# A unit's value products in one row behind all of its transposes, last block of keys first

## The chip, the cores and the metric

The kernel runs on one core of a Trainium2 chip. The metric is the device time of one launch in microseconds; the time before is the median of three runs. Inside a core, TensorE (PE in the profile; PEld is its weight load) multiplies, VectorE (DVE), ScalarE (ACT) and GpSimd (POOL) do the rest, and SyncE (SP) issues the transfers.

## The reference

Two decoder layers over 512 tokens of width 1024. A layer projects the residual stream, runs two kinds of attention side by side, projects their outputs back, normalises, and runs a gated feed-forward part. What matters here are the two kinds of attention:

```python
# kind "a": sliding window of 128 with sinks, 8 query heads, 2 key/value heads
pr = jnp.exp(s - m)
denom = pr.sum(-1, keepdims=True) + jnp.exp(sink - m)
o = jnp.einsum('bnhgqk,bnkhd->bnqhgd', (pr / denom).astype(v.dtype), vv)
# kind "b": the 128 best keys of each query by an indexer's score, 8 query heads, 1 key/value head
_, sel = lax.top_k(idx_score, k_top)
ks, vs = gather(k, sel), gather(v, sel)
pr = jax.nn.softmax(s, axis=-1)
o = jnp.einsum('bqhgj,bqjhd->bqhgd', pr.astype(v.dtype), vs)
```

The kernel doesn't gather: it masks the scores of kind "b" outside the 128 best keys, so both kinds are a masked softmax followed by probabilities times values.

## The kernel before

Tokens are worked on in four tiles of 128. In a layer, `start()` projects the indexer's columns, keys and values and the first queries; `index()` makes the indexer's scores; then three streams are woven into one program order by `Order.run`: `rest()` (the other queries, then the output projection of kind "a" through `from_ma`), `attention()` and `topk()`. Each stream yields the estimated cost of what it has just issued, and the stream with the least accumulated cost goes next. That order is a priority: when the program is built, the framework replays it on a model of the engines, and where an instruction isn't ready on its engine there, a later one that is ready goes ahead. On the chip each engine then runs its own list strictly in order.

Attention is cut into 16 units a layer: kind "a" or "b", a tile t of queries, a group g of four heads. Kind "a" looks at one block of 128 keys (t = 0) or two, kind "b" at t + 1 blocks. `scores` of a unit makes the masked scores (L684, PE), their row minimum (L688, DVE) and the exponentials (L692, ACT); two units later `values` follows, woven step by step with the scores of a later unit. For each block of keys, `values` transposes the four heads' probabilities on PE into a PSUM bank (L721, four 128x128 transposes), copies them to a tile of SBUF (L723, ACT), and multiplies them with the values: `pv(b)` (L715), two matmuls with 64 columns of values as the stationary operand, one for each half of the output's 128 partitions, so each uses half of the array's columns. In float32 a matmul of L715 stands in the trace as two records, so one `pv(b)` is four records. All blocks add into one PSUM accumulator `o`. Then the reciprocals of the sums are transposed (L732) and copied (L735), and DVE scales `o` by them (L740); L747 and L748 split the result in two parts.

Before the change, `pv(b)` is issued `LAG` blocks behind the transposes: one for kind "a", two for kind "b", and the last ones behind L732; after each there is a yield, at which other streams and the scores come in. The copied probabilities lie in `t2k()`, a pool of 12 tiles that also holds the exponentials. `slot()` is another pool, of 28 tiles: keys, queries, values, the outputs of kind "a", and the tiles into which SP loads quarters of `w_down` ahead (L232).

Products of the projections go through `mm3` (L325 to L327), three matmuls over 128 rows and 128 columns of the array.

Of the kernel before, what the change touches and what calls it, by code (L numbers as in the profile page):

```python
# [10 lines left out]
F32 = mybir.dt.float32  # L11
# [24 lines left out]
NSLOT, NTMP = 28, 12  # L36
D_GI, D_KI, D_K, D_Q, AHEAD = 9.0, 13.0, 8.0, 10.0, 2
IDX_PACE, NSTART, R_MAIN, R_TOP = 1.5, 2, 0.75, 0.001
LAG, FILL = dict(a=1, b=2), {2: 6, 5: -2}
QS = [("a", 0), ("a", 1), ("b", 0), ("b", 1)]  # L40


# [54 lines left out]
def hybrid_kernel(ctx: ExitStack, tc: tile.TileContext, x, p, positions, ln_in_g, ln_in_b, w_in,  # L97
# [15 lines left out]
    def bank(tag, bufs, dt=F32):  # L113
        return psum.tile([128, 512], dt, name="bank", tag="bank", bufs=8)

    def acc():
        return bank("acc", 4)

    def slot(dt=F32R):
        return slots.tile([128, 512], dt, name="slot", tag="slot")  # L120

    def t2k(dt=F32):
        return tmp.tile([128, 512], dt, name="t2k", tag="t2k")
# [224 lines left out]
    def tok(t):  # L348
        return slice(t * 128, (t + 1) * 128)
# [198 lines left out]
    for l in range(L):  # L548
# [84 lines left out]
        def wait(*keys):  # L633
            while not all(k in ready for k in keys):
                yield None
# [67 lines left out]
        def values(kind, t, g, st):  # L703

            es, rb, b0, nb = st
            c = g if kind == "a" else 2
            o = acc()[:, :256].rearrange("p (a n) -> p a n", a=2)
            pts = {}
            lag, cost = LAG[kind], 0.45
            if kind == "b":  # L710
                yield from wait("x read")

            def pv(b):
                for u in range(2):
                    PE.matmul(o[u * 64:(u + 1) * 64], vt[b0 + b][:, c * 64:(c + 1) * 64], pts[b][:, u],  # L715
                              start=b == 0, stop=b == nb - 1)

            for b in range(nb):
                ps = bank("tp", 2)
                for j in range(4):  # L720
                    PE.transpose(ps[:, j * 128:(j + 1) * 128], es[j][:, b * 128:(b + 1) * 128], idf)  # L721
                pt = t2k()
                A.copy(pt, ps)  # L723
                pts[b] = pt.rearrange("p (a u n) -> p u a n", a=2, u=2)
                yield 0.44
                if b >= lag:
                    pv(b - lag)
                    yield cost

            pr = bank("tp", 2)  # L730
            for a in range(2):
                PE.transpose(pr[:, a * 128:(a + 1) * 128], rb[:, a * 128:(a + 1) * 128], idf)  # L732
            tt = t2k()
            rr, of = (tt[:, i * 256:(i + 1) * 256].rearrange("p (a n) -> p a n", a=2) for i in range(2))
            A.copy(rr, pr[:, :256].rearrange("p (a n) -> p a n", a=2))  # L735
            yield 0.44
            for b in range(max(0, nb - lag), nb):
                pv(b)
                yield cost
            V.tensor_tensor(of, o, rr, OP.mult)  # L740
            if kind == "a":
                m = ma[t, g] = slot().rearrange("p (s a n) -> p s a n", s=2, a=2)
                hi, lo = m[:, 0], m[:, 1]
            else:
                k = 4 + 2 * g
                hi, lo = fh[:, k:k + 2, tok(t)], fl[:, k:k + 2, tok(t)]
            A.copy(hi, of)  # L747
            G.tensor_tensor(lo, of, hi, OP.subtract)  # L748
            ready.add(("m" + kind, t, g))
# [3 lines left out]
        def attention():  # L753

            st = {}
            for i in range(len(units) + AHEAD):
                gs = []
                if i in FILL:
                    yield 0.0, FILL[i]
                if i < len(units):  # L760
                    st[i] = []
                    gs.append(scores(*units[i], st[i]))
                if i >= AHEAD:
                    gs.append(values(*units[i - AHEAD], st.pop(i - AHEAD)))
                while gs:
                    none = True
                    for g in list(gs):
                        try:
                            c = next(g)
                        except StopIteration:  # L770
                            gs.remove(g)
                            none = False
                            continue
                        if c is not None:
                            none = False
                            yield c
                    if none:
                        yield None
# [230 lines left out]
        for b in TAIL:  # L1009
            for h in range(2):  # L1010
# [18 lines left out]
                for i, t in enumerate(b):  # L1029
                    a = t2k()  # L1030
# [37 lines left out]
```

## Time and profile before

| | us |
|---|---|
| median of 3 runs | 1252.13 (1251.35 to 1252.41) |
| profiled execution | 1251.81, its span 1249.7 |
| PE busy | 1225.9 (98%) |
| DVE, POOL, ACT busy | 765.2, 682.9, 576.4 |
| attention and what is woven with it, layer 1 | about 95 to 218 us of the span |
| the same, layer 2 | about 705 to 830 us of the span |

An engine's busy time is the union of its instructions. A matmul's row spans its way through the array, and successive matmuls overlap, so what a matmul costs is the step from its start to the start of the next one and not the length of its row.

### The profile page before, as it was taken

To read this page: it belongs to the slowest core of one execution; us is meant where nothing else is said; L and a number is where in the kernel's file an instruction comes from. 1 tells how busy PE (TensorE), PEld (TensorE's weight loads), DVE (VectorE), ACT (ScalarE), POOL (GpSimd) and SP (SyncE) were. 2 spreads that over 40 slices of the span, in tenths; PEclk is the share of its full clock that TensorE was granted. 3 is DMA by queue.
4 is the path that set the end of the run, shared out by engine and by line. 5 is a ranking of instruction groups with operands and counts; after the bars stand their busy time and mean duration, and the time that the engine had idled before them with its cause. 6 is when DMAs were issued, how large, how long until landed. Compare 5 with 4: busy or idle time off the path is not lost.

```text
span 1249.7 us, 18006 instructions
## 1 busy us (share of the span) xinstructions
PE 1225.9 (98%) x6552; PEld 1029.9 (82%) x6552; DVE 765.2 (61%) x1678; ACT 576.4 (46%) x1193; POOL 682.9 (55%) x555
## 2 busy tenths in 40 slices
PE   7999999999999999999999999999999999999996
PEld 5998777988888888888899987689888888888885
DVE  7699954682727272726677998286555555555365
ACT  6577763442434343433337787534343333333331
POOL 6885532566566666663169754234757575757400
PEclk9999999999999999999999999999999999999999
DMA  5232311333232323034033203114323333321321
GB/s 177 78 92 85 95 42 35 119 118 118 85 118 84 118 85 118 18 118 140 2 89 114 101 21 117 52 54 149 99 87 105 97 105 99 103 83 52 101 84 50
DMA packets 89264, 112.74 MB, mean 90 GB/s; under 512 B 5460, under 2 KB 66132, under 8 KB 89176
## 3 DMA queue, kind: packets, MB, share of 16 engines
q1 hardware_dynamic: 88504, 111.58, 28.5%
q8 instruction: 51, 0.84, 0.3%
q14 instruction: 37, 0.30, 0.1%
q10 hardware_dynamic: 672, 0.03, 0.0%
HBM read 109.49 MB, written 2.10 MB: 89 GB/s over the span
## 4 chain that ended last, share of the span: by engine, by line
PE 82%; POOL 5%; DVE 3%; issue 3%; ACT 3%; DMA 3%; SPq 0%; DVEq 0%; ACTq 0%; POOLq 0%
PE bank L325 24%; PE bank L326 24%; PE bank L327 24%; PE bank L715 3%; PE bank L684 3%; PE bank L721 2%; POOL wsp L279 2%; DMA wst<-in_w_pg_dram 2%; POOL wsp L257 1%; PE bank L523 1%; PE bank L438 1%; PE bank L732 1%; ACT wsp L278 1%; DVE slot L273 1%; POOL slot L517 1%
## 5 line engine op out<-in xcount | busy, mean ns | idle before, releaser
L279 POOL TENSOR_TENSOR wsp<-wst,wsp 128x1024 fp32r<-128x1024 f32 (+2 forms) x148 | 351.3, 2389 | 244.4 <-ACT wsp L278 240.8
L326 PE MATMUL bank<-fl,wsp 128*128 128x512 f32 (+1 forms) x768 | 284.8, 372 | 0.4 <-DVE fl L441 0.4
L325 PE MATMUL bank<-fh,wsp 128*128 128x512 f32 (+1 forms) x768 | 283.6, 372 | 1.0 <-ACT fh L440 1.0
L327 PE MATMUL bank<-fh,wsp 128*128 128x512 f32 (+1 forms) x768 | 283.1, 371 | 0.0
L278 ACT CAST wsp<-wst 128x1024 fp32r<-128x1024 f32 (+2 forms) x148 | 151.6, 1033 | 166.4 <-PE bank L327 126.2
L325 PE MATMUL bank<-wsp,fh 128*128 128x256 f32 (+3 forms) x512 | 165.2, 326 | 3.6 <-DVE work L648 2.0
L874 DVE TENSOR_TENSOR t2k<-bank,t2k 128x512 f32<-128x512 f32 x44 | 30.4, 692 | 222.0 <-PE bank L327 222.0
L326 PEld LDWEIGHTS bank<-fl,wsp 128*128 128x128 f32 x768 | 144.6, 188 | 25.7 <-DVE fl L441 0.9
L325 PEld LDWEIGHTS bank<-fh,wsp 128*128 128x128 f32 x768 | 143.6, 188 | 26.8 <-ACT fh L440 1.9
L327 PEld LDWEIGHTS bank<-fh,wsp 128*128 128x128 f32 x768 | 144.6, 188 | 24.9
L327 PE MATMUL bank<-wsp,fl 128*128 128x256 f32 (+3 forms) x512 | 163.7, 322 | 1.4 <-DVE fl L441 0.8
L326 PE MATMUL bank<-wsp,fh 128*128 128x256 f32 (+3 forms) x512 | 164.7, 322 | 0.0
L257 POOL TENSOR_TENSOR wsp<-slot,wsp 128x512 fp32r<-128x512 f32 x100 | 141.6, 1442 | 29.0 <-ACT wsp L256 29.0
L325 PE MATMUL bank<-wsp,slot 128*128 128x512 f32 x392 | 153.8, 392 | 0.0
L326 PE MATMUL bank<-wsp,slot 128*128 128x512 f32 x392 | 152.7, 390 | 0.0
L327 PE MATMUL bank<-wsp,slot 128*128 128x512 f32 x392 | 148.4, 390 | 0.0
L790 DVE TENSOR_TENSOR x<-bank,x 128x512 f32<-128x512 f32 x140 | 91.5, 684 | 88.5 <-PE bank L327 88.5
L904 ACT CAST slot<-t2k 128x256 fp32r<-128x256 f32 (+1 forms) x104 | 49.8, 497 | 144.1 <-DVE t2k L874 102.5
L257 POOL TENSOR_TENSOR wsp<-t2k,wsp 128x512 fp32r<-128x512 f32 x40 | 57.5, 1448 | 92.4 <-ACT wsp L256 92.4
L325 PEld LDWEIGHTS bank<-wsp,fh 128*128 128x128 f32 x512 | 97.6, 191 | 11.9 <-ACT fh L440 2.4
L327 PEld LDWEIGHTS bank<-wsp,fl 128*128 128x128 f32 x512 | 97.5, 191 | 7.9 <-DVE fl L441 1.1
L326 PEld LDWEIGHTS bank<-wsp,fh 128*128 128x128 f32 x512 | 98.0, 191 | 6.5 <-issue 1.2
(152 smaller groups left out, 2004.6 us busy)
## 6 DMA issues: line engine op xcount, KB each, us to landing
wst<-in_w_gu_dram SPq DMA_DIRECT2D x88, 512.0 KB, 3.5
slot<-in_w_down_dram SPq DMA_DIRECT2D x80, 256.0 KB, 2.8
wst<-in_w_in_dram SPq DMA_DIRECT2D x16, 512.0 KB, 3.6
wst<-in_w_o_dram SPq DMA_DIRECT2D x16, 512.0 KB, 3.8
wst<-in_w_pg_dram SPq DMA_DIRECT2D x16, 512.0 KB, 4.2
wst<-in_w_in_dram SPq DMA_DIRECT2D x8, 256.0 KB, 2.7
lng<-in_ln_g_dram SPq DMA_DIRECT2D x4, 512.0 KB, 4.8
lnb<-in_ln_b_dram SPq DMA_DIRECT2D x4, 512.0 KB, 5.5
```

The source lines that it names most:

```text
L257: G.tensor_tensor(w[:, 1, j], src[j], w[:, 0, j], OP.subtract)
L278: A.copy(w[:, 0, :a * n], st[:, :a * n])
L279: G.tensor_tensor(w[:, 1, :a * n], st[:, :a * n], w[:, 0, :a * n], OP.subtract)
L325: PE.matmul(o, sh, mh, start=start, stop=False, skip_group_check=again)
L326: PE.matmul(o, sh, ml, start=False, stop=False, skip_group_check=again)
L327: PE.matmul(o, sl, mh, start=False, stop=stop, skip_group_check=again)
L684: PE.matmul(ps[:, o:o + nn], qT[kind, t, g][:, j * 128:(j + 1) * 128], kT[c, s][:, k0:k0 + nn], start=(s == 0), stop=(s == 1))
L715: PE.matmul(o[u * 64:(u + 1) * 64], vt[b0 + b][:, c * 64:(c + 1) * 64], pts[b][:, u], start=b == 0, stop=b == nb - 1)
L721: PE.transpose(ps[:, j * 128:(j + 1) * 128], es[j][:, b * 128:(b + 1) * 128], idf)
L790: V.tensor_tensor(xt[t][:, c], ps, xt[t][:, c], OP.add)
L874: V.tensor_tensor(a, ps[1, f], a, OP.mult)
L904: A.copy(h[0], src)
```

## The change

`LAG` goes. In `values` all blocks are transposed and copied first, then come the reciprocals' transposes (L732) and their copy, and behind them all `pv(b)` of the unit without a yield between, from the last block to the first; the accumulation starts with the last block and stops with the first. For kind "b" the copied probabilities move from `t2k()` to `slot()`, since up to four of them live at once. The yields are 0.44 for each block, 0.22 behind L732 and 0.2 + 0.45 per block behind the products; before they were 0.44 for each block, 0.44 behind L732 and 0.45 behind each product.

```diff
-LAG, FILL = dict(a=1, b=2), {2: 6, 5: -2}
+FILL = {2: 6, 5: -2}
...
-            lag, cost = LAG[kind], 0.45
...
             def pv(b):
                 for u in range(2):
                     PE.matmul(o[u * 64:(u + 1) * 64], vt[b0 + b][:, c * 64:(c + 1) * 64], pts[b][:, u],
-                              start=b == 0, stop=b == nb - 1)
+                              start=b == nb - 1, stop=b == 0)
 
             for b in range(nb):
                 ps = bank("tp", 2)
                 for j in range(4):
                     PE.transpose(ps[:, j * 128:(j + 1) * 128], es[j][:, b * 128:(b + 1) * 128], idf)
-                pt = t2k()
+                pt = slot(F32) if kind == "b" else t2k()
                 A.copy(pt, ps)
                 pts[b] = pt.rearrange("p (a u n) -> p u a n", a=2, u=2)
                 yield 0.44
-                if b >= lag:
-                    pv(b - lag)
-                    yield cost
...
-            yield 0.44
-            for b in range(max(0, nb - lag), nb):
+            yield 0.22
+            for b in reversed(range(nb)):
                 pv(b)
-                yield cost
+            yield 0.2 + 0.45 * nb
```

## Rows read from the trace of the kernel before

**Rows 1.** The page: busy time of PE, and its granted clock in 40 slices.
```profile
PE 1225.9 (98%) x6552; PEld 1029.9 (82%) x6552; DVE 765.2 (61%) x1678; ACT 576.4 (46%) x1193; POOL 682.9 (55%) x555
...
PEclk9999999999999999999999999999999999999999
```
**Rows 2.** The page: the chain that ended last, shares of the span by line.
```profile
PE bank L325 24%; PE bank L326 24%; PE bank L327 24%; PE bank L715 3%; PE bank L684 3%; PE bank L721 2%; POOL wsp L279 2%; DMA wst<-in_w_pg_dram 2%; POOL wsp L257 1%; PE bank L523 1%; PE bank L438 1%; PE bank L732 1%; ACT wsp L278 1%; DVE slot L273 1%; POOL slot L517 1%
```
**Rows 3.** PE's waits in both attention stretches: total us, times, longest.
```profile
PE bank L684 <- ACT slot L524: 0.6, 1, 0.6
...
PE bank L684 <- ACT slot L524: 0.8, 1, 0.8
PE bank L715 <- ACT t2k L723: 0.2, 1, 0.2
```
**Rows 4.** Windows: busy us (instructions) of PE, PEld, DVE, ACT, POOL; PEclk.
```profile
95.00:218.00 123.00, 122.21 (x794) 95.67 (x793) 87.44 (x288) 78.67 (x225) 51.05 (x73) 1.00 0.20 64
705.00:830.00 125.00, 123.82 (x808) 97.42 (x808) 91.17 (x299) 81.97 (x234) 51.45 (x73) 1.00 0.19 62
802.00:809.00 7.00, 7.00 (x50) 4.37 (x49) 1.11 (x2) 5.06 (x10) 5.17 (x4) 1.00 0.35 105
```
**Rows 5.** Groups of PE by line and shape: busy us, mean ns, idle before.
```profile
L715 PE MATMUL bank<-t2k,slot 128*64 128x256 f32 x272 | 42.6, 402 | 0.4 <-ACT t2k L723 0.2
```
**Rows 6.** Timeline of PE, layer 2: start us, length us, line, records.
```profile
809.06 0.40 PE L327 MATMUL bank<-wsp,fl 128*128 128x512 f32 x1
809.29 0.40 PE L325 MATMUL bank<-wsp,fh 128*128 128x512 f32 x1
...
810.22 0.39 PE L326 MATMUL bank<-wsp,fh 128*128 128x512 f32 x1
810.54 1.08 PE L715 MATMUL bank<-t2k,slot 128*64 128x256 f32 x8
811.55 0.50 PE L327 MATMUL bank<-wsp,fl 128*128 128x512 f32 x1
811.89 0.40 PE L325 MATMUL bank<-wsp,fh 128*128 128x512 f32 x1
...
813.37 0.65 PE L715 MATMUL bank<-t2k,slot 128*64 128x256 f32 x4
813.95 0.50 PE L325 MATMUL bank<-wsp,fh 128*128 128x512 f32 x1
```
**Rows 7.** Timeline of PE: value products between transposes.
```profile
804.00 0.27 PE L721 MATMUL bank<-idf,t2k 128*128 128x128 f32 x1
804.20 0.65 PE L715 MATMUL bank<-t2k,slot 128*64 128x256 f32 x4
804.78 0.87 PE L721 MATMUL bank<-idf,t2k 128*128 128x128 f32 x6
```
**Rows 8.** Timeline of PE: sixteen transposes in a row, and what follows.
```profile
616.21 1.91 PE L438 MATMUL bank<-idf,x 128*128 128x128 f32 x16
617.87 0.47 PE L325 MATMUL bank<-wsp,fh 128*128 128x512 f32 x1
618.19 0.39 PE L326 MATMUL bank<-wsp,fh 128*128 128x512 f32 x1
```
**Rows 9.** Timeline of PE: the first run of value products.
```profile
104.81 0.65 PE L715 MATMUL bank<-t2k,slot 128*64 128x256 f32 x4
105.39 0.39 PE L326 MATMUL bank<-wsp,fh 128*128 128x256 f32 x1
```
**Rows 10.** Waits, whole span: value products behind the copies.
```profile
PEld bank L715 <- ACT t2k L723: 2.8, 8, 0.7
```
**Rows 11.** Timeline: a one-block unit's copy and product, then a copy-bound pair.
```profile
763.48 0.59 ACT L723 COPY t2k<-bank 128x512 f32<-128x512 f32 x1 [1.04 <-PE bank L721]
764.12 0.65 PE L715 MATMUL bank<-t2k,slot 128*64 128x256 f32 x4
...
779.82 0.65 PE L715 MATMUL bank<-t2k,slot 128*64 128x256 f32 x4
780.69 0.65 PE L715 MATMUL bank<-t2k,slot 128*64 128x256 f32 x4 [0.22 <-ACT t2k L723]
```
**Rows 12.** SP in layer 1: quarters of w_down, and what they waited for.
```profile
141.73 13.64 SPq L232 DMA_DIRECT2D slot<-in_w_down_dram  x8
...
SPq L232 <- PE bank L684: 5.8, 1, 5.8
SPq L232 <- PE bank L732: 3.3, 1, 3.3
```
**Rows 13.** Timeline of PE near the start: eight transposes.
```profile
12.19 1.97 PE L438 MATMUL bank<-idf,x 128*128 128x128 f32 x8 [2.04 <-DVE x L400]
```

## The prediction

> **What bounds the kernel now.** I read the page's busy times first, then its chain, then PE's waits in the two attention stretches, then single steps of the timeline. PE is busy 98% of the span, at a granted clock of nine tenths or more in every slice [rows 1]. The chain that ended last runs over PE's product lines; the lines of attention stand in it too, L715 with 3%, L684 with 3%, L721 with 2% [rows 2]. In the two stretches that the change touches, PE is busy 122.2 of 123 and 123.8 of 125 us [rows 4], and its waits for other engines come to 0.6 us in the first and 1.0 us in the second [rows 3]. DVE and ACT have 29% and 36% of the first stretch free [rows 4]. So nothing there is faster than PE's own list of instructions: PE is the bound, and what PE spends on an instruction or between two of them comes off or goes on the time one for one. The reader should see that a busy PE isn't a PE without loss: a row spans a matmul's whole way, so a loss of 0.1 us between two matmuls hides under the rows. It shows only in the steps from start to start.
>
> **The change part by part.** The number of matmuls stays. L715 keeps its 272 records [rows 5]: 68 block products, 34 a layer, four records each.
>
> *What one run of value products costs.* A product between two others of 512 columns starts 0.23 us after the one before (809.06 to 809.29). Where a run of L715 begins, the step is 0.32 (810.22 to 810.54), 0.09 more. A run of four records lasts from 813.37 to 813.95, 0.58; one of eight from 810.54 to 811.55, 1.01. Four more records, one more block, thus cost 0.43, and a run has 0.58 - 0.43 = 0.15 on top whatever its length. Behind it the next product takes 0.34 instead of 0.23 (811.55 to 811.89), 0.11 more [rows 6]. Fixed cost of a run among products: 0.09 + 0.15 + 0.11 = 0.35 us. Among transposes: sixteen of them and the step behind take 618.19 - 616.21 - 0.23 = 1.75, so 0.109 each [rows 8]; from a transpose to L715 the step is 0.20, 0.09 more; the run has its 0.15; and the six transposes behind it have a row of 0.87, where a row of six by rows 8 would have 1.91 - 10 x 0.109 = 0.82, 0.05 more [rows 7]. Together 0.29. It is the change from full-width matmuls to half-width ones and back that is paid, once for each run.
>
> *How many runs go.* I counted maximal sequences of L715 among all of PE's matmuls, from 104.81 [rows 9] to 813.37 [rows 6]: 58 runs, 29 in each layer, 48 of one block and 10 of two. With the products of a unit in one row there are as many runs as units, 16 a layer, 32 in all. 26 runs go. Ends: 26 x 0.29 = 7.5 us and 26 x 0.35 = 9.1 us. About two fifths of the sides of the 58 runs are transposes, so I take 0.32: **8.3 us** less.
>
> *The transposes*, which now stand closer together, earn nothing of their own: sixteen cost 1.75 with both ends, as many as their 0.109 each, so moving into and out of them costs next to nothing [rows 8].
>
> *The new wait.* The first product of a row needs the copy of the last block, and that copy has ACT's queue before it. PE's list is strict: behind a waiting L715 stand the projections of `rest()` or the tail's products, and behind them DVE's additions, which are in no hurry. Before, waits of L715 for copies were 8, with 2.8 us of idle weight load in all, longest 0.7, and part of that is the run's fixed cost [rows 10]; on PE itself only 0.2 us is named [rows 3]. In the steps, two blocks back to back should be 0.43 apart, and the pair at 779.82 and 780.69 is 0.87 apart: a wait of 0.44, the longest I found. The arrangement to come stands already in the trace in the eight units of one block, whose only product follows their only copy: at 764.12 the product starts 0.05 behind the copy's end [rows 11], at the price of some 0.1 us; one other of the eight does so as well, six have slack. For 24 units of several blocks the ends are -0.9 (the 2.8 of rows 10, less 8 x 0.24 that belong to the runs themselves, go and nothing comes) and 24 x 0.44 = 10.6; I take the nearest row, the units of one block: 24 x 2/8 x 0.1 = 0.6, and say **+0.7 us**.
>
> *Copies in `slot()`.* Kind "b" has 20 copies a layer. No row shows how many of the 28 tiles are free, but SP's loads of `w_down` into them went out over 13.64 us with waits of 5.8 and 3.3 us for matmuls that gave a tile back [rows 12]: the pool is full at the time when kind "b" begins, and the copies will compete with those loads. A copy that comes late delays only L715 of its unit as long as `rest()` has products to put between. For the loads a delay is covered: they are wanted in the feed-forward part, past 218 us. Ends: -1 (twelve tiles of `t2k()` get some relief) and 2 x (3.3 + 5.8) = 18; I take 0, since a unit of kind "b" gives its own copies back within a few us and PE has other work; the upper end has a rival of its own below.
>
> *Yields.* A unit's sum changes by 0.02, so the share of the streams stays; in lumps of up to 2 us the other streams catch up a little later. I cost it at nothing, since PE has work of either stream; without that cover it is a step of 0.1 or 0.2 us in a unit. The last unit of a layer has all its products later, but the tail of the output projection takes tile 3 last, so three tiles with 24 products of 0.23 each, 16 us, lie before it [rows 6].
>
> *Sum:* 1251.81 - 8.3 + 0.7 = 1244.2 for the profiled execution, which is 0.3 below the median: **1244.5 us**. The feed-forward part keeps its time: PE gives weight buffers back in it at the same pace.
>
> **The rivals.** (a) *The rows are broken.* The order is made on a model of the engines; a score or a turn of queries that is ready there and of higher priority slips between the products. For it: L715 runs in before were split wherever something else was ready. Against it: ten runs of two blocks stayed whole even across a yield. If half of the 26 stay split: 1252.1 - 4.2 + 0.4 = 1248.3. (b) *The wait at the head takes the place of the switches; slower.* Place: PE's queue in front of each row of several blocks, price 0.44 as at 780.69. It decides from 8.3 / 24 = 0.35 us a unit. At the full 0.44: 1252.1 - 8.3 + 10.6 = 1254.4. For it: a row begins with the youngest copy instead of the oldest. Against it: in before, too, products stood right behind a copy's end, and PE's named waits for L723 came to 0.2 us [rows 3]. (c) *The tiles.* Copies wait for `slot()` where `rest()` has run dry, 3.3 us a layer by rows 12: 1252.1 - 8.3 + 6.6 = 1250.4. (d) *The clock.* With up to 18 transposes together, PE may drop to its lower level, as near the start, where eight transposes take about as long as sixteen later [rows 8, 13]. If the last two units of each layer (36 transposes, 3.9 us) doubled, it would cost 7.8: 1252.1 - 8.3 + 0.7 + 7.8 = 1252.3. The Trainium skill, page "TensorE: Matmul & The Clock Gate", Part 4, says that transposes don't count as busy for the clock in the way of products. The trace speaks against it: from 802 to 809, nearly all transposes and value products, the clock is 1.00 [rows 4], and the product behind sixteen transposes runs at the full pace after one longer step [rows 8].
>
> **How the numbers follow.** Forecast 0.68, (a) 0.14, (b) 0.07, (c) 0.06, (d) 0.02, others 0.03. A measurement tells 0.2%, 2.5 us, from no change. Faster: forecast and (a) whole, 0.83 with some of the rest; same: (c) and (d), 0.09; slower: (b) and others, 0.08. The forecast's own range goes from 1241.5 (9.1, the 0.9 of waits and a little relief) to 1247. For 8 in 10 I go up over (a) to 1250, and leave (b) and part of (c) out.
>
> **What would show it.** 32 runs of L715 instead of 58, with lengths of 4, 8, 12 and 16 records, each lasting 0.43 per block + 0.15; both attention stretches about 4 us shorter and the rest of the span as it was; waits of L715 for L723 few and under 0.5 us; PE still busy 98%. It is wrong if runs stay near 58, if a run of sixteen takes over 2.0 us, if PE's idle time in the stretches grows by more than 4 us, or if SP's loads of `w_down` push PE's weights out.

## The result and the profile after

The changed kernel takes 1258.58 us (median of 6 runs, 1256.96 to 1259.71) where the kernel before takes 1251.89: a ratio of 1.0053 (95% interval 1.0040 to 1.0066), 6.7 us slower. The profiled execution has a span of 1256.6 us against 1249.7.

The page of after, busy times and the chain by line; they answer to [rows 1] and [rows 2]:

```profile
PE 1221.7 (97%) x6552; PEld 1034.7 (82%) x6552; DVE 765.9 (61%) x1678; ACT 575.9 (46%) x1193; POOL 682.4 (54%) x555
...
PE bank L325 25%; PE bank L326 25%; PE bank L327 25%; PE bank L714 3%; PE bank L684 2%; PE bank L720 1%; DMA wst<-in_w_pg_dram 1%; POOL wsp L279 1%; ACT t2k L692 1%; ACT slot L722 1%; ACT wsp L278 1%; PE bank L438 1%; POOL slot L517 1%; PE bank L523 1%; DVE slot L273 1%
```

L714 is the former L715 (value products), L720 the former L721 (transposes), L722 the former L723 (copies), L728 the former L732 (transposes of the reciprocals), L736 the former L740, L743 the former L747 (the cast of a unit's result). PE is busy 4.2 us less in a span that is 6.9 us longer, and ACT's copies and exponentials have entered the chain. The groups of L714 say why (columns as in [rows 5]), and so do PE's waits in the two attention stretches, which answer to [rows 3]:

```profile
L714 PE MATMUL bank<-slot 128*64 128x256 f32 x160 | 20.8, 389 | 7.0 <-ACT slot L722 7.0
L714 PE MATMUL bank<-t2k,slot 128*64 128x256 f32 x112 | 16.9, 395 | 1.7 <-ACT t2k L722 1.7
...
PE bank L714 <- ACT slot L722: 3.7, 4, 1.3
PE bank L684 <- DVE ng L688: 1.0, 1, 1.0
PE bank L714 <- ACT t2k L722: 0.7, 2, 0.4
...
PE bank L714 <- ACT slot L722: 3.4, 4, 1.4
PE bank L728 <- POOL rb L700: 1.5, 2, 1.2
PE bank L714 <- ACT t2k L722: 1.0, 2, 0.7
PE bank L684 <- DVE ng L688: 0.8, 1, 0.8
PE bank L684 <- ACT slot L524: 0.5, 1, 0.5
```

The value products wait for their copies twelve times, 8.7 us in all; before it was 0.2 us. The last unit of layer 1 shows one such wait whole (timeline, ACT and PE):

```profile
196.57 1.97 PE L720 MATMUL bank<-idf,t2k 128*128 128x128 f32 x16
...
197.26 0.59 ACT L722 COPY slot<-bank 128x512 f32<-128x512 f32 x1 [1.42 <-PE bank L720]
197.75 0.41 ACT L743 CAST fh<-t2k 128x256 fp32r<-128x256 f32 x1
198.06 1.56 ACT L722 COPY slot<-bank 128x512 f32<-128x512 f32 x3
...
198.38 0.38 PE L728 MATMUL bank<-idf,rb 128*128 128x128 f32 x2
...
199.67 1.95 PE L714 MATMUL bank<-slot 128*64 128x256 f32 x16 [0.91 <-ACT slot L722]
201.55 0.50 PE L325 MATMUL bank<-wsp,fh 128*128 128x512 f32 x1
```

Sixteen transposes leave PE in 1.8 us. The four copies, with one cast (L743) between them, last from 197.26 to 199.62. PE has two more transposes in its list (L728), then the row, whose first product needs the fourth copy. From 198.38 two steps of 0.11 would have led to about 198.7, with the usual step into a run; the row starts at 199.67. The products of the output projection, which need no copy of this unit, stand behind the row (201.55). The row itself is as cheap as forecast: sixteen records in 201.55 - 199.67 = 1.88 us, where 4 x 0.43 + 0.15 is 1.87.

In the two units with the longest waits ACT has exponentials of a later unit's scores (L692) between the copies. One of them, a row of three blocks whose last transpose ended at 183.53:

```profile
184.22 0.72 ACT L692 ACTIVATE t2k<-t2k,ng 128x512 f32<-128x512 f32 x1
...
184.93 0.57 ACT L722 COPY slot<-bank 128x512 f32<-128x512 f32 x1
...
185.55 1.52 PE L714 MATMUL bank<-slot 128*64 128x256 f32 x12 [1.34 <-ACT slot L722]
```

### The profile page after: what moved, and what is told of

Its sections match the earlier page's. It is cut to its first block, busy times and chain, and to the rows that moved or that the text cites. A ratio compares the mean times of both kernels' runs of the same rounds, so it can differ in the third digit from the quotient of the medians.

```text
span 1256.6 us, 18000 instructions
## 1 busy us (share of the span) xinstructions
PE 1221.7 (97%) x6552; PEld 1034.7 (82%) x6552; DVE 765.9 (61%) x1678; ACT 575.9 (46%) x1193; POOL 682.4 (54%) x555
## 4 chain that ended last, share of the span: by engine, by line
PE 84%; ACT 5%; DVE 4%; POOL 3%; issue 2%; DMA 2%; SPq 0%; ACTq 0%; DVEq 0%; POOLq 0%
PE bank L325 25%; PE bank L326 25%; PE bank L327 25%; PE bank L714 3%; PE bank L684 2%; PE bank L720 1%; DMA wst<-in_w_pg_dram 1%; POOL wsp L279 1%; ACT t2k L692 1%; ACT slot L722 1%; ACT wsp L278 1%; PE bank L438 1%; POOL slot L517 1%; PE bank L523 1%; DVE slot L273 1%
## 5 line engine op out<-in xcount | busy, mean ns | idle before, releaser
L327 PE MATMUL bank<-fh,wsp 128*128 128x512 f32 (+1 forms) x768 | 283.1, 371 | 0.0
L327 PEld LDWEIGHTS bank<-fh,wsp 128*128 128x128 f32 x768 | 144.6, 188 | 25.2
L327 PE MATMUL bank<-wsp,fl 128*128 128x256 f32 (+3 forms) x512 | 163.7, 323 | 1.3 <-DVE fl L441 0.8
L327 PE MATMUL bank<-wsp,slot 128*128 128x512 f32 x392 | 148.4, 389 | 0.0
L327 PEld LDWEIGHTS bank<-wsp,fl 128*128 128x128 f32 x512 | 97.8, 192 | 7.6 <-DVE fl L441 1.1
```

The costliest lines, as they stand in the source:

```text
L327: PE.matmul(o, sl, mh, start=False, stop=stop, skip_group_check=again)
```

## The experiments

Each kernel is measured beside the kernel before on the same chip. "Runs" are maximal sequences of value products in PE's steps, counted as in the prediction. "Head waits" are the steps into a run over the usual one, summed over both layers: 0.4 us before, 9.6 us after.

**First to last.** One thing of the change undone:

```diff
-                              start=b == nb - 1, stop=b == 0)
+                              start=b == 0, stop=b == nb - 1)
...
-            for b in reversed(range(nb)):
+            for b in range(nb):
```

> The changed kernel with one thing undone: the products of a unit run from the first block of keys to the last. Theory W (the head of each row waits for ACT's copy of the last block, and that eats the saved switches): the first product needs the oldest copy, so the wait moves behind products or is filled, and the rows break up; PE's built order has 56 runs of value products instead of 34, so about 22 x 0.32 = 7 us of switches come back and about 8 of the 10 us of waits go: 1251 to 1255 us. Rival S (the copies of kind b are late because they wait for tiles of the slot pool, whatever the order of products): waits stay and switches come back, 1262 to 1266 us. Rival C (the loss is the clock or the order of other work): within 2 us of 1258.

Measured: 1254.78 us, ratio 1.0015 (1.0006 to 1.0024). 56 runs, head waits 1.0 us. As theory W has it: the direction is what makes the rows whole and what makes their heads wait. Taken alone this undoes both, and the kernel is back near the one before. Six of its ten times hold, by their mean clock, a fall of the clock worth about 2 us (last section); the other four are 1252.7 to 1253.3.

**The copies back in `t2k`.** The line `pt = slot(F32) if kind == "b" else t2k()` becomes `pt = t2k()`.

> The changed kernel with the copies of kind b back in the pool of 12 temporary tiles; PE's built order is nearly that of the changed kernel, 34 runs. Theory W: the pool doesn't matter, 1257 to 1260 us, and the waits at the heads of the rows stay at 8 to 11 us in all. Rival S (tiles of the slot pool are what the copies wait for): the waits fall under 4 us and the time to 1249 to 1252 us.

Measured: 1256.41 us, ratio 1.0036 (1.0022 to 1.0049); 34 runs. The products still wait for copies twelve times, 8.7 us:

```profile
PE bank L714 <- ACT t2k L722: 8.7, 12, 1.3
```

The time is 0.6 us under what W expected, the waits for copies are W's. The products don't wait for the pool. The time is 2.2 us under the changed kernel's, though: in the second attention stretch PE no longer has the 1.5 us of waits at L728, so inside the changed kernel the pool may cost something by the order that it leads to. That is not tested further. The next run puts the pool alone into the kernel before.

**The kernel before with the copies of kind "b" in `slot`.** The same line, put into the kernel before.

> The kernel before with only the copies of kind b moved to the slot pool. Theory W: nothing, 1251 to 1253.5 us. Rival S (tiles): 1255 us or more.

Measured: 1251.90 us, ratio 1.0000 (0.9991 to 1.0010). This part of the change is worth nothing by itself.

**Odd blocks copied by VectorE.**

```diff
-                A.copy(pt, ps)
+                (V.tensor_copy if b % 2 else A.copy)(pt, ps)
```

> The changed kernel with the copies of odd blocks on VectorE instead of ScalarE: four copies no longer stand one behind the other. PE's built order has 32 runs, and the heads stand as close behind the transposes as in the changed kernel. Theory W: where two engines copy, a row of four blocks waits some 1.0 us less; units whose last block is even still wait for ScalarE, and VectorE has a queue of its own; waits in all 4 to 8 us instead of 10: 1250 to 1256 us. Rival S: the copies wait for tiles as before, 1257 to 1260 us.

Measured: 1256.39 us, ratio 1.0035 (1.0021 to 1.0049). Head waits 7.8 us, inside what W gave them, the time just outside. The waits went down where VectorE copied, but PE then waited for VectorE elsewhere:

```profile
PE bank L684 <- DVE ng L688: 4.0, 4, 1.6
PE bank L714 <- ACT slot L722: 3.9, 5, 1.4
...
PE bank L714 <- DVE slot L722: 1.7, 3, 0.6
```

Dividing the copies between two engines is not the cure; it takes VectorE's time from the row minimum of the next scores (L688), and those feed PE as well.

**The scores between the transposes and the row.** In `attention`, a unit's transposes and L728 are issued first, then the later unit's scores, then the row; the last two rows come behind both units' transposes.

```diff
-                while gs:
...
+                last = i >= len(units)
+                if i >= AHEAD:
+                    row[i] = gs.pop()
+                    for c in row[i]:
+                        yield c
+                        if c == 0.22:
+                            break
+                for g in gs:
+                    yield from g
+                if i >= AHEAD and not last:
+                    yield from row.pop(i)
+            for i in sorted(row):
+                yield from row.pop(i)
```

> The changed kernel, but a unit's transposes are issued first, then the scores of the later unit, then the row of products; the last two units' rows stand behind both units' transposes. PE's built order has 30 runs, and between the last transpose and the row 0.9 to 7.5 us of other PE work stand, where the changed kernel has 0.2 to 0.7 for ten units. Theory W: the saved switches (28 x 0.32 = 9 us) stay, the waits at the heads fall from 10 us to 1 to 3: 1244 to 1248 us. Rival S or C: little changes, 1255 to 1260 us.

Measured: 1254.38 us, ratio 1.0021 (1.0012 to 1.0030). 30 runs, as theory W said, and head waits of 0.6 us, even under its 1 to 3, but a time that neither theory gave. PE's waits, first and second attention stretch:

```profile
PE bank L728 <- POOL rb L700: 4.4, 3, 2.3
PE bank L523 <- DVE ng L688: 0.8, 1, 0.8
PE bank L684 <- ACT slot L524: 0.8, 1, 0.8
PE bank L714 <- DVE work L660: 0.4, 1, 0.4
...
PE bank L728 <- POOL rb L700: 3.6, 4, 1.3
PE bank L684 <- ACT slot L524: 1.4, 1, 1.4
```

The waits have moved to L728, the transposes of the reciprocals. Those need the sums of the exponentials, VectorE's reciprocal and GpSimd's broadcast (L700), and with the transposes brought forward they came before that chain was through: 8.0 us by these lists, 9.5 by the steps into L728. The granted clock in this profile also fell twice in the first attention stretch (see the last section); that stretch is 4.6 us longer than in the kernel before, and the second, without a fall, is as long as before.

**The same with L728 behind the scores too.** A mark after the last block's yield, and the break at the mark.

```diff
                 yield 0.44
+            yield 1e-9
...
-                        if c == 0.22:
+                        if c == 1e-9:
                             break
```

> As the run with the scores between, but the reciprocals' two transposes (they wait for GpSimd's broadcast of the sums) come behind the scores too, right in front of the row. In the run before they stood right behind the unit's transposes, and PE waited there 9.5 us in all (2.42 the longest), which gave back what the heads of the rows no longer waited. Theory W, widened (PE's list has no slack behind a unit's transposes; whatever needs another engine there waits): these waits fall to 1 to 3 us, the clock no longer falls in attention, 27 rows less keep 26 x 0.32 = 8 us: 1244 to 1248 us. Rival M (PE's waits only move to the next instruction that needs another engine, as attention's chain through ACT and DVE is as long as PE's list): 1251 to 1255 us, waits on PE in the attention stretches still 8 us or more.

Measured: 1244.54 us, ratio 0.9941 (0.9929 to 0.9954): 7.4 us faster than the kernel before and 14 us faster than the changed kernel. I call this kernel the fast version below. 33 runs, head waits 0.4 us. PE's waits in the two stretches:

```profile
PE bank L684 <- ACT slot L524: 1.0, 1, 1.0
PE bank L684 <- DVE ng L688: 0.4, 1, 0.4
PE bank L325 <- DVE t2k L737: 0.2, 1, 0.2
...
PE bank L684 <- ACT slot L524: 0.9, 1, 0.9
```

The last two units of layer 1, to be held against the timeline above; L729 is here what L728 is there:

```profile
189.75 0.93 PE L720 MATMUL bank<-idf,t2k 128*128 128x128 f32 x7
190.43 0.48 PE L325 MATMUL bank<-wsp,slot 128*128 128x512 f32 x1
...
191.67 0.38 PE L729 MATMUL bank<-idf,rb 128*128 128x128 f32 x2
191.98 1.95 PE L714 MATMUL bank<-slot 128*64 128x256 f32 x16
193.86 0.50 PE L327 MATMUL bank<-wsp,slot 128*128 128x512 f32 x1
194.20 0.38 PE L729 MATMUL bank<-idf,rb 128*128 128x128 f32 x2
194.51 1.95 PE L714 MATMUL bank<-slot 128*64 128x256 f32 x16
196.38 0.50 PE L325 MATMUL bank<-wsp,fh 128*128 128x512 f32 x1
```

The rows are the same sixteen records, but between the last block's transposes and the first row stand 1.2 us of other products and L729, and no step waits. Rival M, that PE's waits only move from one instruction to the next, falls: it described the version before and not this one.

**Full-width value products.** In the kernel before, so that the order stays and the width changes (with it goes the split of a block over two halves of the array):

```diff
-                    PE.matmul(o[u * 64:(u + 1) * 64], vt[b0 + b][:, c * 64:(c + 1) * 64], pts[b][:, u],
-                              start=b == 0, stop=b == nb - 1)
+                    PE.matmul(o.rearrange("p (a n) -> p a n", a=2), vt[b0 + b][:, 0:128], pts[b][:, u],
+                              start=b == 0 and u == 0, stop=b == nb - 1 and u == 1)
```

> The kernel before, with the value products over 128 columns of the stationary operand instead of 64, both halves adding into the same accumulator: it leaves out which half of the output a head pair belongs to, so its output is not the reference's. A block then costs 4 x 0.216 = 0.86 us instead of 0.43, since the halves no longer run side by side. If a run's fixed cost is the change between half width and full width, the steps into and out of a run fall to 0.23 and 0.23 among products of 512 columns and the run has nothing on top: 68 x 0.43 - 58 x 0.32 = +10.7, 1261 to 1265 us. If it belongs to float32 operands or to the accumulator whatever the width, the steps stay at 0.32 and 0.34: 1278 to 1284 us.

Measured: 1262.78 us, a single time, inside the first of the two ranges. Timeline of PE, to be held against [rows 6]:

```profile
819.28 0.39 PE L327 MATMUL bank<-wsp,fl 128*128 128x512 f32 x1
819.51 1.89 PE L715 MATMUL bank<-t2k,slot 128*128 128x256 f32 x8
821.04 0.58 PE L325 MATMUL bank<-wsp,fh 128*128 128x512 f32 x1
821.46 0.40 PE L326 MATMUL bank<-wsp,fh 128*128 128x512 f32 x1
```

The step into the run is 0.23, as between two products of L327; from the run's start to the second product behind it are 821.46 - 819.51 = 1.95 us, which is 8 x 0.216 + 0.23. Nothing is left over, where the half-width run of eight has 811.89 - 810.54 = 1.35 for 0.86 + 0.23, and 0.09 ahead of it [rows 6]. The fixed cost of a run belongs to the change between half width and full width.

**Transposes first, but no row.** The fast version with a yield of 0.45 behind each product, and the products alternating with the scores as in the kernel before.

> As the fast version (transposes, scores of the later unit, reciprocals' transposes, row), but the products are not in a row: each has a yield behind it and they alternate with the scores. The transposes still come early. PE's built order has 45 runs of value products instead of 33. Theory W (two separate terms: 0.32 us for each run, and the waits at what follows the transposes): 12 x 0.32 = 3.8 us more, 1247 to 1250 us. Rival (the gain comes from the earlier transposes alone, the rows don't matter): 1243.5 to 1246 us.

Measured: 1259.30 us, ratio 1.0059 (1.0047 to 1.0072): a miss, by 9 us over W's upper end and further over the rival's. It has the 45 runs, worth 3.8 us. What was not expected: the waits came back, since L729 and the first products stood early again. PE's waits over the span, the largest of those of attention:

```profile
PE bank L684 <- DVE ng L688: 3.8, 4, 1.3
PE bank L714 <- ACT slot L722: 3.3, 4, 1.3
...
PE bank L729 <- POOL rb L700: 2.7, 4, 1.1
```

Of the 14.8 us over the fast version, the runs are 3.8 and named waits in the attention stretches 9.2 (11.7 against 2.5): theory W's two terms, of which it priced only the first. So early transposes alone bring nothing here. The run doesn't isolate the price of a switch, because two things moved.

**The fast version, first to last.**

> The fast version with the products from the first block to the last. PE's built order has 42 runs instead of 33, since the oldest copy is ready first and the model lets other work in behind it. Theory W: 9 x 0.32 = 2.9 us more, 1246 to 1249 us, waits as in the fast version. Rival (the direction matters beyond the number of runs): under 1246 or over 1250 us.

Measured: 1247.40 us, ratio 0.9965 (0.9951 to 0.9979). 42 runs, head waits 0.5 us, and 2.9 us more than the fast version, as W had it. The size is in part luck, as the stretches of the profiles show. They are bounded by the starts of the same instructions in every kernel (last L645 of the indexer and first L438 behind attention; first and last L645 of layer 2's indexer), and the numbers are us against the kernel before:

| | attention, layer 1 | indexer, layer 2 | attention, layer 2 |
|---|---|---|---|
| changed kernel | +1.5 | +2.0 | +3.6 |
| fast version | -3.9 | +0.5 | -3.8 |
| fast version, first to last | -2.9 | +2.0 | -2.8 |

Attention is 2.0 us longer than in the fast version, 0.22 us for each of the nine runs. Another 1.5 us lie in the indexer, which has no value products: there the granted clock fell in this profile and not in that of the fast version (last section). With slack in front of the row, the direction costs no more than the runs that it adds; the price of a run is not measured by this pair.

## Why the prediction was wrong

I forecast 1244.5 us and 1241 to 1250; it was 1258.6. Point by point:

- *PE is the bound, and its steps count one for one.* Right, but for the clock, which took 1.7 us in the profile of the changed kernel (last section).
- *What a run costs, and how many go.* Right in kind and size. Forecast were 32 runs and 0.32 us; there are 34 (two rows of two blocks were broken). The price comes back in the fast version: 25 runs fewer than the kernel before, and its attention stretches are 7.7 us shorter, 0.31 for each run, with named waits of 2.5 us there against 1.6. These are also the "about 4 us" for each stretch that the prediction gave as its sign. That the change of width is what is paid, argued from steps alone, is shown by the full-width run.
- *The new wait.* **This step failed.** It took 0.7 us, from the units of one block; by the same count of steps it is 9.2 us (9.6 against 0.4 before), more than the 24 x 0.32 = 7.7 that the runs gave back. The longest wait is 1.4, where the upper end of my price was 0.44. The nearest row was the wrong one. A one-block unit has two score steps of the later unit between its transposes and its product. In a unit of three or four blocks the transposes have used these steps up or nearly so, the last two units have no later scores at all, and in the new order hardly more than L728 is left in front of the row. In PE's list of the changed kernel 0.2 to 0.7 us of other work stand there for six of the eight units of three and four blocks, 1.2 to 6.7 for most other units; the six longest head waits (0.93 to 1.44 us, 7.0 of the 9.6) are those six units. The rates of the two engines are not the reason: three copies together take 1.56, so they start about 0.48 apart, and four transposes at 0.109 take PE 0.44. What the step left out is, first, that the last copy still takes its own 0.6 behind the last transposes, which two transposes of 0.11 don't cover, and second, what else stands in ACT's list between the copies: in four of the six units the cast L743, which puts the next copy off by 0.31, and in the other two, those with the longest waits (1.41 and 1.44), exponentials of 0.72 each.
- *"PE has work of either stream."* This was the same fault in another place, the sentence on the yields. PE had the work, but behind the row in its list, and the list is strict. Work covers a wait only if it stands in front of the waiting instruction.
- *Copies in `slot()`.* Right at 0, by the run of the kernel before with that part alone; inside the changed kernel an effect of up to 2.2 us is open.
- *Rival (b)* named the place (PE's queue in front of each row of several blocks) and the point from which it decides, 0.35 us a unit; I gave it 0.07 and 1254.4 us. Its mechanism is what happened, with 9.2 / 24 = 0.38 a unit, over that point. *Rival (a)*: seen only as two broken rows. *Rival (c)*: the products' waits for copies stay with the other pool, so it is not what made them wait. *Rival (d)*: the clock fell, but not in the transposes, see below.
- *The sum of after.* Its span is 6.9 us longer, of which 5.1 lie in the two attention stretches and 2.0 in layer 2's indexer, where the clock took 1.7. In the stretches -7.7 (runs) + 9.2 (heads) + 2.4 (what the other named waits grew by: L684 and L728 in the lists above, against [rows 3]) make 3.9 of the 5.1; about 1.2 us are not assigned. So in this profile the change itself lost about 5 us, and the clock the rest. The median is made of times that differ by up to 2.8 us, at mean granted clocks of 0.996 to 0.998 that don't sort them.

The forecast's own number came true only in the version that gives the row its slack: 1244.54.

## What to carry to other kernels

Bringing instructions of one kind together saves the switches between kinds, but it brings together their waits too: what was a lag of one or two blocks between a product and its copy became none. Before pricing such a move, count for each kind of unit how much of the engine's own work stands, in its list, between the last producer and the first consumer, and compare it with the time that the other engine needs for its last instruction and for what else stands in its own list there; then put independent work there (here the later unit's scores, and behind them everything else that needs a third engine). When a wait is cured and the time stays, look for the next instruction in the list that needs another engine, since curing one of two gave 4 us of the 14.

## What the runs showed of the hardware

A run of half-width matmuls among full-width ones costs PE 0.29 to 0.35 us by its steps (0.31 by whole stretches), seen for runs of 4, 8 and 16 records, though the two halves run side by side and a block then takes 0.43 instead of 0.86 us. I had read this from steps before; that it vanishes wholly at full width was new.

The granted clock fell inside the span in some profiles. In that of after, windows around the start of layer 2's indexer (busy us of PE, PEld, DVE, ACT, POOL; then PEclk), and the same place in the fast version and in the fast version from first to last, then two windows of the first attention stretch in the kernel with the scores between:

```profile
669.00:672.00 3.00, 1.84 (x15) 1.26 (x13) 1.86 (x5) 3.00 (x11) 3.00 (x3) 1.00 0.43 110
672.00:676.00 4.00, 3.96 (x20) 3.96 (x21) 3.63 (x13) 3.22 (x12) 3.55 (x3) 0.57 0.77 213
...
665.00:668.00 3.00, 1.80 (x11) 1.33 (x11) 2.52 (x8) 3.00 (x15) 3.00 (x2) 1.00 0.71 180
668.00:672.00 4.00, 4.00 (x35) 4.00 (x34) 3.89 (x13) 3.25 (x10) 3.81 (x3) 1.00 0.86 240
...
665.00:668.00 3.00, 1.79 (x13) 1.26 (x12) 2.29 (x7) 3.00 (x13) 3.00 (x2) 1.00 0.60 167
668.00:672.00 4.00, 4.00 (x23) 4.00 (x22) 3.60 (x11) 2.90 (x11) 3.77 (x3) 0.57 0.76 216
...
132.00:136.00 4.00, 3.55 (x18) 2.95 (x20) 3.93 (x11) 2.49 (x10) 2.04 (x5) 0.58 0.01 4
149.00:153.00 4.00, 4.00 (x18) 2.64 (x19) 4.00 (x12) 2.05 (x8) 3.31 (x4) 0.59 0.30 74
```

PE waited alike in the first three, busy 1.8 of 3 us, and the clock fell in two of them, to a mean of 0.57 of 2.4 GHz over four microseconds, that is to 1.2 GHz for most of them; 4 x 0.43 = 1.7 us were lost. The profile with the copies in `t2k` has the same fall at the same place (0.58 from 673 to 677), those of the kernel before, of the changed kernel from first to last and of the odd blocks on VectorE have none there. It was a stretch with waits that the fall followed, not the transposes that the prediction's last rival had in mind: the bursts of sixteen transposes in after (196.57 above) ran at full pace. In the kernel with the scores between, the first fall lies right behind its longest wait, the 2.25 us that end at 132.45 with L728.

What a fall costs can also be seen in the times of the changed kernel from first to last: six of ten had a mean granted clock of 0.996 and took 1254.7 to 1255.0 us, the other four 0.997 to 0.998 and 1252.7 to 1253.3. Why the clock falls in one execution and not in another with the same waits stays open.
